# Sixteen narrow tiles in one batch, float16 pairs of queries and keys, and eight weight slots in an encoder trunk

## The chip, the cores and the metric

One Trainium2 chip, one of its cores. The metric is the device time of one execution in microseconds. The engines are named as in the profile: PE (matrix products), DVE (vector), ACT (activations), POOL (GpSimd), SP (issues the DMAs). PEld is PE's loading of the stationary operand, which overlaps with PE.

## The reference

Two layers over 2048 positions of 1024 features. In each layer one input projection feeds a gated spatial mixer (group A) and an attention with eight query heads on two key heads (group B); their outputs together go through one output projection, are normalised and added to x.

```python
for l in range(DEPTH):                                   # DEPTH = 2
    h = rmsnorm(x, pre_g[l])
    proj = jnp.einsum('bsd,de->bse', h, w_in[l])
    u_a, v_a, g_a, q, k, v, g_b = jnp.split(proj, idx, axis=-1)
    y_a = gmlp_group(u_a, v_a, ln_a_g[l], ln_a_b[l], spatial_w[l], spatial_b[l]) * jax.nn.silu(g_a)
    y_b = gqa_axial_attention(q, k, v, q_norm_g[l], k_norm_g[l], tables) * jax.nn.silu(g_b)
    out = jnp.einsum('bse,ed->bsd', jnp.concatenate([y_a, y_b], axis=-1), w_out[l])
    x = x + rmsnorm(out, post_g[l])
# inside the attention, for a block of queries:
    q = apply_axial_rope(rmsnorm(q, qn_g)); k = apply_axial_rope(rmsnorm(k, kn_g))
    sc = jnp.einsum('bqkgd,bskd->bkgqs', qblk, k).astype(jnp.float32) * HEAD_DIM ** -0.5
    p = jax.nn.softmax(sc, axis=-1)
    o = jnp.einsum('bkgqs,bskd->bqkgd', p, v)
```

The inputs' q_norm_g and k_norm_g are drawn around 8, so scores are large and the softmax is sharp.

## The kernel before

Values are kept to nearly float32 by splitting them: a value is the sum of a high and a low part, and a product of two values is made of three products of parts (PASSES). The type float32r, which PE takes at full rate, holds the parts in most places; the attention weights are split into float16 parts.

A layer has two stages. In the **projection stage**, weights come from memory in blocks of 256 columns (load_w, tile w_raw), are scaled and split on ACT and DVE (split_w, tiles w_hi and w_lo), and are multiplied with the transposed input hT. Work that hangs on a block's result is put in a list of delayed jobs (Background) and issued between matmuls: do_kv normalises keys, rotates them and transposes them into k_st and k_lo; do_q does it for queries and stores their two parts to memory (q_d). The pool big holds hT, the keys, the values (v_st) and later the output weights (wo); the pool wp ("w" slots) holds weights, and in the attention p_parts, p_f and y_t; the pool fp ("f" slots) holds tiles of 512 columns.

In the **attention stage** a unit is a block of 512 queries and a head: 32 units a layer, in the order of their blocks. A unit has sixteen steps, one for a tile of 128 keys, so a layer has 512 steps. attend() writes the steps out in one loop over k, and its engines' instructions are kept in that order (Pinned). In step k:

- PE makes the scores sp of tile k from two products: k_st, which holds the keys' high part twice over, with the queries' two parts stacked (s.qs, tile q_st), and k_lo, the keys' low part and a row of ones, with the queries' high part and the row of subtracted maxima (s.q2, tile q2; the order prints it as q_ and a number).
- ACT makes the exponential twice from sp: p_parts (high part, float16) and p_f (float32). POOL, or DVE for 15 of 100 steps, subtracts them to the low part, again p_parts.
- Between, PE makes a maximum product pmax for a later unit (DVE reduces it to mx) and some products of an output projection (pout), which stand in a list called fill.
- PE multiplies the high part of step k - 3 with the values (po, 128 columns of weights), and at the end of every BATCH steps the narrow products of the batch: for each tile two of 32 columns with the low part (po) and two that sum both parts (sums, with one_h). These four stand in different column groups of the array.

The tiles sp, pmax, pout, po, and the small t, pd, pg come from one pool of seven PSUM banks (ps_t). After a unit's last batch, finish() queues what divides by the sums: half and whole join po's two halves (o_pair), den_t and den bring the sums over (den, pd), gate scales the gate gb by them, gate_t and mul apply it, split makes the two parts of y and stores them to y_d.

The maxima only have to be near the true ones, since they divide out; EXP_SHIFT is added to their negative, so that exponentials use float16's range. They go to memory (m_d) as a row of 512.

Of the kernel before, what the change touches and what calls it, by code (L numbers as in the profile page):

```python
# [9 lines left out]
F32 = mybir.dt.float32  # L10
F32R = mybir.dt.float32r
# [27 lines left out]
def encoder(ctx: ExitStack, tc, x, w_in, w_out, pre_g, post_g, ln_a_g, ln_a_b,  # L39
# [18 lines left out]

    def big_t(shape, name):
        return big.tile(shape, F32R, name=name, tag="big")  # L60

# [36 lines left out]
    one_h = const.tile([P, 32], F16, name="one_h")  # L98
    nc.vector.memset(one_h, 1.0)
# [3 lines left out]
    q_d = [dram.tile([NH, 2, HD, GRP], F32, name=f"q_d{g}") for g in range(NG)]  # L103
    m_d = [dram.tile([NH, GRP], F32, name=f"m_d{g}") for g in range(NG)]
    gb_d = [dram.tile([P, TPG, NH * HD], F32, name=f"gb_d{g}") for g in range(NG)]
# [69 lines left out]
    class Project:  # L175
# [23 lines left out]

# [160 lines left out]
        def do_kv(self, g, banks):  # L360
            k_st, k_lo, v32, _ = self.kv
            b4 = [ps.rearrange("p (t h d) -> p t h d", t=2, d=HD) for ps in banks]
            for i, ps in enumerate(b4):
                t = g * TPG + 2 * i
                nc.scalar.copy(v32[:, t:t + 2], ps[:, :, 2:4])
            krs = self.norm_rope([ps[:, :, 0:2] for ps in b4], NKV, self.rope_rows(g, self.gain_k))
            for i, kr in enumerate(krs):
                for j in range(2):
                    t = g * TPG + 2 * i + j
                    kk = f_t("kk", 3 * NKV * HD).rearrange("p (k a d) -> p k a d", k=NKV, a=3)  # L370
                    nc.scalar.copy(kk[:, :, 0, :].bitcast(F32R), kr[:, j])
                    nc.scalar.copy(kk[:, :, 1, :], kk[:, :, 0, :])
                    nc.gpsimd.tensor_tensor(kk[:, :, 2, :], kr[:, j], kk[:, :, 0, :], ALU.subtract)

                    def trans(t=t, kk=kk):
# [4 lines left out]
                        nc.scalar.copy(k_st[:, :, t * P:(t + 1) * P],  # L380
                                       pk[:, 0:2 * P].rearrange("p (k s) -> p k s", k=NKV))
                        nc.vector.tensor_copy(k_lo[0:HD, :, t * P:(t + 1) * P],
                                              pk[0:HD, 2 * P:4 * P].rearrange("p (k s) -> p k s", k=NKV))
                    bg.add(KK_DELAY + 2 * (2 * i + j), trans)

        def do_q(self, g, banks, b):
            qrs = self.norm_rope([ps.rearrange("p (t h d) -> p t h d", t=2, d=HD) for ps in banks], 4,
                                 self.rope_rows(g, self.gain_q))
            for i, qr in enumerate(qrs):
                def trans(i=i, qr=qr):  # L390
                    ps = ps_t("pt").rearrange("p (k t) -> p k t", k=2)
                    for t in range(2):
                        for k in range(2):
                            PE.transpose(ps[:, k, t * P:(t + 1) * P], qr[:, t, 2 * k:2 * k + 2, :], ident)
                    hi = f_t("fh", dt=F32R).rearrange("p (k t) -> p k t", k=2)
                    lo = f_t("fl", dt=F32R).rearrange("p (k t) -> p k t", k=2)
                    nc.scalar.copy(hi, ps)
                    nc.vector.tensor_tensor(lo, ps, hi.bitcast(F32), ALU.subtract)
                    for a, part in enumerate((hi, lo)):
                        for h in range(2):  # L400
                            dst = q_d[g][4 * b + h:4 * b + 4:2, a, :, i * 2 * P:(i + 1) * 2 * P]
                            nc.sync.dma_start(dst.rearrange("k d t -> d k t"),
                                              part.bitcast(F32)[h * HD:(h + 1) * HD])
                bg.add(Q_DELAY + 2 * i, trans)
# [202 lines left out]
    LAG_LO = 3  # L607
    BATCH = 8
    N_HI = 12
    N_F = 4  # L610
    N_LO = 12
    LAST_0 = 5
# [3 lines left out]
    def attend(l, kv, nxt):  # L616
# [31 lines left out]
        def load_qm(u):  # L648
            qb, h = units[u]
            s = state[u]  # L650
            s.qm = f_t("q_m", dt=F32R)
            nc.sync.dma_start(s.qm.bitcast(F32), q_d[qb][h].rearrange("a d t -> (a d) t"))
            s.mx = small.tile([P, TPG, NG], F32, name="mx", bufs=3)

        def load_q(u):
            qb, h = units[u]
            s = state[u]
            s.qs = f_t("q_st", dt=F32R)
            nc.sync.dma_start(s.qs.bitcast(F32), q_d[qb][h].rearrange("a d t -> (a d) t"))
            s.q2 = f_t("q2", dt=F32R)  # L660
            nc.sync.dma_start(s.q2.bitcast(F32)[0:HD], q_d[qb][h, 0])
            nc.sync.dma_start(s.q2.bitcast(F32)[HD:HD + 1], m_d[qb][h:h + 1])

# [13 lines left out]
        def stack_max(u, pe, act):  # L677
# [3 lines left out]
            pe.transpose(ps[0:TPG, 0:P], s.m, ident)  # L681
            rows = small.tile([TPG, P], F32R, name="m_rows")
            act.activation(rows, ps[0:TPG, 0:P], AF.Copy, bias=EXP_SHIFT)
            nc.sync.dma_start(m_d[qb][h].rearrange("(t p) -> t p", p=P), rows.bitcast(F32))

        def finish(u, k):
# [65 lines left out]
            at(k + BATCH + 3, gate_t)  # L752
            at(k + BATCH + 4, mul)
            at(k + BATCH + 5, split)

# [250 lines left out]
        yield before, first_wo  # L1006
        both = [w_t([P, 8, GRP], "p_parts", F16) for _ in range(3)]
        both = [b[:, n] for b in both for n in range(8)]
# [64 lines left out]
        for k in range(end + 4):  # L1073
            if k < total:
                u, i = k // NT, k % NT
                s = state[u]
                kv = units[u][1] // (NH // NKV)
                if i == 0 and units[u][1] % 2 == 0:
                    load_gb(u)
# [30 lines left out]
            if 0 <= kb < total:  # L1110
                u, i = kb // NT, kb % NT
                s = state[u]
                kv = units[u][1] // (NH // NKV)
                if i % BATCH == BATCH - 1:
                    while narrow:
                        narrow.pop(0)()
                    for n in range(i - BATCH + 1, i + 1):
                        kn = kb - i + n
# [7 lines left out]
                if i == NT - 1:  # L1126
                    finish(u, k + 1)
                    if units[u][1] == NH - 1 and u + 1 < len(units):
                        fill_to = min(k + 16 + NH * NT, total - LAST_0)
                        at(k + 16, lambda qb=units[u][0]: fill.extend(out_steps(qb)))  # L1130
        assert not later
# [30 lines left out]
    for l in range(DEPTH):  # L1162
        kv = [big_t([P, NKV, S], "k_st"), big_t([P, NKV, S], "k_lo")]
# [49 lines left out]
```

## Time and profile before

| | us |
|---|---|
| median of three runs | 2810.36 |
| lowest and highest | 2807.75, 2815.12 |
| the profiled execution's own time | 2813.78 |
| its span, first to last instruction | 2812.0 |
| first score product of layer 0 and of layer 1 | 626.7, 2016.5 |
| last score product of layer 0 and of layer 1 | 1388.0, 2773.7 |

The profile is one execution with each instruction's start and end. A row of a list of groups gives the source line (L84 is the helper that records all pinned instructions, so groups are told apart by tiles), the engine, the operation, what it writes and reads, the shapes, how often, the busy time in us, the mean of one in ns, and behind the last bar the idle time of the engine just before them with what ended it. A row of the view in order of time begins with start and duration in us, and merges like instructions that follow each other (x8). The granted clock of PE was 0.99 of full over the execution.

### The profile page before, as it was taken

To read this page: it belongs to the slowest core of one execution; us is meant where nothing else is said; L and a number is where in the kernel's file an instruction comes from. 1 tells how busy PE (TensorE), PEld (TensorE's weight loads), DVE (VectorE), ACT (ScalarE), POOL (GpSimd) and SP (SyncE) were. 2 spreads that over 40 slices of the span, in tenths; PEclk is the share of its full clock that TensorE was granted. 3 is DMA by queue.
4 is the path that set the end of the run, shared out by engine and by line. 5 is a ranking of instruction groups with operands and counts; after the bars stand their busy time and mean duration, and the time that the engine had idled before them with its cause. 6 is when DMAs were issued, how large, how long until landed. Compare 5 with 4: busy or idle time off the path is not lost.

```text
span 2812.0 us, 49354 instructions
## 1 busy us (share of the span) xinstructions
PE 2738.1 (97%) x18294; PEld 2067.2 (74%) x18294; DVE 1894.9 (67%) x3976; ACT 1583.3 (56%) x3295; POOL 1300.1 (46%) x1112
## 2 busy tenths in 40 slices
PE   7999999999999999999999999999999999999997
PEld 7998899885556666566699989998755666666665
DVE  7863788876666666666497639798766555656654
ACT  5322432228887777777642225322478877777774
POOL 1210121018776676666532111200377766767665
PEclk9999999999999999999999999999999999999999
DMA  4533433422222232232345343342322232221323
GB/s 134 165 110 108 137 108 90 124 90 97 85 85 89 94 91 97 87 100 89 139 151 151 122 128 121 102 124 91 112 68 94 78 100 71 83 92 59 115 71 127
DMA packets 276563, 293.71 MB, mean 104 GB/s; under 512 B 20450, under 2 KB 214306, under 8 KB 276324
## 3 DMA queue, kind: packets, MB, share of 16 engines
q1 hardware_dynamic: 276324, 290.57, 33.1%
q8 instruction: 145, 2.38, 0.3%
q14 instruction: 94, 0.77, 0.1%
HBM read 197.02 MB, written 93.45 MB: 103 GB/s over the span
## 4 chain that ended last, share of the span: by engine, by line
PE 79%; DVE 12%; ACT 4%; issue 2%; DMA 1%; POOL 1%; SPq 0%; DVEq 0%; POOLq 0%; ACTq 0%
PE pp L84 25%; PE sp L84 16%; PE pout L84 12%; PE po L84 12%; PE pmax L84 7%; PE sums L84 4%; PE pt L84 2%; DVE fc L346 2%; DVE w_lo L253 2%; ACT p_parts L84 1%; ACT p_f L84 1%; DMA w_raw<-in_w_in_dram 1%; DVE mx L670 1%; DVE o_t L84 1%; DVE fb L435 1%
## 5 line engine op out<-in xcount | busy, mean ns | idle before, releaser
L84 POOL TENSOR_TENSOR p_parts<-p_f,p_parts 128x512 f16<-128x512 f32 x872 | 1038.7, 1207 | 438.9 <-ACT p_f L84 256.7
L84 ACT ACTIVATE p_parts<-sp 128x512 f16<-128x512 f32 x1024 | 627.6, 613 | 334.5 <-PE sp L84 323.1
L84 DVE TENSOR_REDUCE mx<-pmax 128x1 f32<-128x512 f32 x768 | 515.0, 683 | 314.2 <-PE pmax L84 312.3
L84 PE MATMUL po<-p_parts,v_st 128*32 128x512 f16 (+1 forms) x3072 | 638.9, 383 | 0.0
L84 ACT ACTIVATE p_f<-sp 128x512 f32<-128x512 f32 x1024 | 629.3, 615 | 0.0
L84 PE MATMUL sp<-q_st,k_st 128*128 128x512 f32 x1024 | 578.7, 565 | 4.5 <-DVE mx L84 3.5
L84 PE MATMUL pp<-w_hi,hT 128*128 128x256 f32 x3584 | 494.8, 287 | 15.6 <-DVE hT L293 8.1
L84 PE MATMUL pout<-wo,y_t 128*128 128x512 f32 x1488 | 494.2, 397 | 0.0
L84 PEld LDWEIGHTS pp<-w_hi,hT 128*128 128x128 f32 x3584 | 461.1, 194 | 21.9 <-DVE hT L293 8.7
L84 PEld LDWEIGHTS <-v_st 128*32 128x32 f16 (+1 forms) x3072 | 193.0, 96 | 328.6 <-issue 287.4
L84 PE MATMUL pmax<-k_st,q_m 128*128 128x512 f32 x1024 | 409.7, 402 | 5.3 <-DVE mx L84 2.6
L84 PE MATMUL sp<-q,k_lo 65*128 65x512 f32 x1024 | 403.3, 394 | 0.0
L84 PEld LDWEIGHTS pout<-wo,y_t 128*128 128x128 f32 x1488 | 280.3, 189 | 60.8 <-DVE mx L84 1.7
L455 POOL TENSOR_TENSOR fl<-fa,fh 128x512 fp32r<-128x512 f32 x32 | 42.1, 1315 | 516.8 <-ACT fh L454 445.2
L84 PE MATMUL pp<-w_lo,hT 128*128 128x256 f32 x1792 | 262.4, 289 | 2.4 <-DVE w_lo L253 2.2
L84 PE MATMUL pp<-hT,w_hi 128*128 128x512 f32 x1024 | 257.8, 390 | 0.0
L84 PEld LDWEIGHTS sp<-q_st,k_st 128*128 128x128 f32 x1024 | 202.8, 198 | 65.2 <-issue 42.5
L84 PEld LDWEIGHTS pp<-w_lo,hT 128*128 128x128 f32 x1792 | 237.3, 194 | 6.6 <-DVE w_lo L253 4.8
L84 PE MATMUL sums<-p_parts,one_h 128*32 128x512 f16 x2048 | 241.8, 379 | 0.0
L252 ACT ACTIVATE w_hi<-w_raw,g_pre 128x256 fp32r<-128x256 f32 x352 | 151.8, 500 | 153.7 <-DMA w_raw<-in_w_in_dram 108.9
L84 PEld LDWEIGHTS pmax<-k_st,q_m 128*128 128x128 f32 x1024 | 193.4, 189 | 56.7 <-DVE mx L84 4.5
L84 PEld LDWEIGHTS pp<-hT,w_hi 128*128 128x128 f32 x1024 | 191.7, 188 | 39.7
(153 smaller groups left out, 3085.1 us busy)
## 6 DMA issues: line engine op xcount, KB each, us to landing
w_raw<-in_w_in_dram SPq DMA_DIRECT2D x28, 1024.0 KB
y_t<-y_d SPq DMA_DIRECT2D x56, 512.0 KB
w_raw<-in_w_in_dram SPq DMA_DIRECT2D x32, 512.0 KB
q_m<-q_d SPq DMA_DIRECT2D x64, 256.0 KB
q_st<-q_d SPq DMA_DIRECT2D x64, 256.0 KB
x_t<-in_x_dram SPq DMA_DIRECT2D x16, 512.0 KB
q_d<-fh SPq DMA_DIRECT2D x64, 128.0 KB
q_d<-fl SPq DMA_DIRECT2D x64, 128.0 KB
```

Source lines behind the costliest of these rows:

```text
L84: return tc.keep_in_program_order(call(*args, **kw))
L252: nc.scalar.activation(hi[:, d], raw[:, d], AF.Copy, scale=g)
L253: nc.vector.scalar_tensor_tensor(lo[:, d], raw[:, d], g, hi.bitcast(F32)[:, d], ALU.mult, ALU.subtract)
L346: nc.vector.tensor_tensor(t2[:, :, :, lo:lo + 16], qn[:, :, :, hi:hi + 16], tbi[:, :, 1:2, lo:lo + 16].broadcast_to([P, 2, n, 16]), ALU.mult)
L435: nc.vector.scalar_tensor_tensor(s.zt[r, c, :], pz[r, h * P:(h + 1) * P], self.lng[r, c:c + 1], self.zbias[r, c, :], ALU.mult, ALU.add)
L455: nc.gpsimd.tensor_tensor(lo, th, hi.bitcast(F32), ALU.subtract)
L670: dve.tensor_reduce(s.mx[:, j, c:c + 1], ps, AX.X, ALU.max)
```

## The change

Queries and keys are split into float16 parts instead of float32r ones, so q_d, m_d, q_m, q_st, q2 and the keys halve in size. k_st and k_lo become halves of one tile k_t, and the pool big goes from seven to six slots, the pool wp from six to eight. The room in wp goes to p_parts: five tiles instead of three, for 20 high and 20 low parts instead of 12 and 12, and the narrow products come in batches of sixteen tiles (BATCH), except in a layer's last three units (BATCH_END, eight). What finish() queues by the batch's length moves with it, load_gb too, and the output projection's steps enter fill at k + 24 instead of k + 16.

So that the parts fit float16, both gains are divided by a power of two near their largest value (gains). Its product and the factor HEAD_DIM ** -0.5 become a column, unit, by which the exponential scales the scores; EXP_SHIFT becomes a column, shift, which it adds. The keys' low part is now the difference of the transposed key in PSUM and its high part, made by DVE, and no longer transposed by itself; the ones row of k_lo is set by DVE instead of a DMA.

```diff
-    big = ctx.enter_context(tc.tile_pool(name="big", bufs=7))
-    wp = ctx.enter_context(tc.tile_pool(name="wp", bufs=6))
+    big = ctx.enter_context(tc.tile_pool(name="big", bufs=6))
+    wp = ctx.enter_context(tc.tile_pool(name="wp", bufs=8))
...
+    shift = const.tile([P, 1], F32, name="shift")
+    nc.vector.memset(shift, EXP_SHIFT)
...
-            nc.vector.tensor_scalar_mul(self.gain_q, self.gain_q, HD ** -0.5)
+            for i, gain in enumerate((self.gain_q, self.gain_k)):
+                nc.vector.tensor_reduce(top[:, i, 0:1], gain[:, 0], AX.X, ALU.max)
+                nc.vector.tensor_reduce(top[:, i, 1:2], gain[:, 0], AX.X, ALU.min, negate=True)
...
+            for i, gain in enumerate((self.gain_q, self.gain_k)):
+                nc.vector.tensor_scalar(gain, gain, inv[:, i:i + 1], None, ALU.mult)
+            self.unit = lay.tile([P, 1], F32, name="unit", bufs=2)
+            nc.vector.tensor_scalar(self.unit, e[:, 0:1], e[:, 1:2], HD ** -0.5, ALU.mult, ALU.mult)
...
                         for k in range(NKV):
-                            PE.transpose(pk[:, k * P:(k + 1) * P], kk[:, k, 0:2, :], ident)
-                            PE.transpose(pk[0:HD, (2 + k) * P:(3 + k) * P], kk[:, k, 2, :], ident)
+                            PE.transpose(pk[:, k * P:(k + 1) * P], kk[:, NKV * j + k], ident)
...
+                        nc.scalar.copy(k_st[:, :, tt], pk)
+                        nc.vector.tensor_tensor(k_lo[0:HD, :, tt], pk[0:HD], k_st[0:HD, :, tt], ALU.subtract)
...
-    BATCH = 8
-    N_HI = 12
+    BATCH, BATCH_END = 16, 8
+    N_HI = 20
...
-            s.qm = f_t("q_m", dt=F32R)
+            s.qm = f_t("q_m", dt=F16)
...
-            at(k + BATCH, rden)
-            at(k + BATCH + 1, gate)
+            n = batch(u + 1)
+            at(k + n, rden)
+            at(k + n + 1, gate)
             if side == 0:
+                at(k + n - 8, lambda: load_gb(u))
                 return
...
+        def batch(u):
+            return BATCH_END if u >= len(units) - 3 else BATCH
...
-                ACT.activation(p_hi(k), sp, AF.Exp)
-                ACT.activation(p_f(k), sp, AF.Exp)
+                ACT.activation(p_hi(k), sp, AF.Exp, bias=shift, scale=layers[l].unit)
+                ACT.activation(p_f(k), sp, AF.Exp, bias=shift, scale=layers[l].unit)
...
-                if i % BATCH == BATCH - 1:
+                size = batch(u)
+                if i % size == size - 1:
...
-                        at(k + 16, lambda qb=units[u][0]: fill.extend(out_steps(qb)))
+                        at(k + BATCH + 8, lambda qb=units[u][0]: fill.extend(out_steps(qb)))
...
-        nc.sync.dma_start(kv[1].bitcast(F32)[HD:HD + 1].rearrange("p k (n i) -> p (k n) i", i=P),
-                          ones1.unsqueeze(1).broadcast_to([1, NKV * S // P, P]))
+        nc.vector.memset(kv[1][HD:HD + 1], 1.0)
```

ACT's queue where the first layer's attention begins (fa and fh are the last gates of the projection stage, t and m_rows a unit's row of maxima, wo the output weights). Before:

```order
L634 CAST wo<-wo_raw 128x512 x2
L683 ACTIVATE m_rows<-t_7043 4x128
L448 ACTIVATE fa<-pp 128x512
L454 CAST fh<-fa 128x512
L84 ACTIVATE p_parts<-sp 128x512
L84 ACTIVATE p_f<-sp 128x512
```

In the changed kernel:

```order
L646 CAST wo<-wo_raw 128x512 x2
L695 CAST m_rows<-t_6985 4x128
L460 ACTIVATE fa<-pp 128x512
L466 CAST fh<-fa 128x512
L84 ACTIVATE p_parts<-sp,shift,unit 128x512
L84 ACTIVATE p_f<-sp,shift,unit 128x512
```

Nothing moved between them; each exponential reads two more operands, and the row of maxima no longer adds the shift.

PE's queue in the attention, one step and the start of a batch, before:

```order
L84 MATMUL sp<-q_st,k_st 128x512
L84 MATMUL sp<-q_23489,k_lo 128x512
L84 MATMUL pout<-wo,y_t 128x512
L84 LDWEIGHTS v_st
L84 MATMUL po<-p_parts,v_st 128x512
L84 LDWEIGHTS v_st
L84 MATMUL po<-p_parts,v_st 32x512
```

In the changed kernel:

```order
L84 LDWEIGHTS k_t
L84 MATMUL sp<-q_st,k_t 128x512
L84 LDWEIGHTS k_t
L84 MATMUL sp<-q_st,k_t 128x512
L84 MATMUL pout<-wo,y_t 128x512
L84 LDWEIGHTS v_st
L84 MATMUL po<-p_parts,v_st 128x512
L84 MATMUL pd<-den,two_v 32x4 x4
L84 LDWEIGHTS v_st
L84 MATMUL po<-p_parts,v_st 32x512
```

The score products have rows of their own for their weights (float32r products load theirs without one). The last row shown is the first of 32 narrow products (32x512) before, and of 64 now. Over the program 128 batches of 32 become 58 of 64 and 12 of 32.

DVE's queue early in the first layer's projection stage, before:

```order
L283 TENSOR_SCALAR x_t<-x_t,rs_x 128x512 x2
L133 TENSOR_SCALAR rs_m<-ss_x 128x1
L198 TENSOR_SCALAR gain_q<-gain_q 128x128
L134 TENSOR_SCALAR rs_x<-rs_m 128x1
L293 TENSOR_TENSOR hT<-pt,hT 128x4x128
L136 TENSOR_SCALAR rs_t<-rs_x,rs_m 128x1
L253 SCALAR_TENSOR_TENSOR w_lo<-w_raw,g_pre,w_hi 128x256
```

In the changed kernel:

```order
L299 TENSOR_SCALAR x_t<-x_t,rs_x 128x512 x2
L135 TENSOR_SCALAR rs_m<-ss_x 128x1
L1184 MEMSET k_t 1x4096
L136 TENSOR_SCALAR rs_x<-rs_m 128x1
L204 TENSOR_REDUCE g_top<-gain_q 128x1
L138 TENSOR_SCALAR rs_t<-rs_x,rs_m 128x1
L205 TENSOR_REDUCE g_top<-gain_q 128x1
L139 TENSOR_SCALAR rs_x<-rs_t,rs_x 128x1
L206 TENSOR_TENSOR g_exp<-g_top 128x2
L269 SCALAR_TENSOR_TENSOR w_lo<-w_raw,g_pre,w_hi 128x256
```

The ones row (MEMSET k_t) and the work on the gains (g_top and what follows) now stand in DVE's queue ahead of the splits of weights (w_lo) and of the input's low parts (hT) that follow.

More of the change, by code (lines that the diff above doesn't have):

```diff
@@ L57, in encoder, with big_t @@
     dram = ctx.enter_context(tc.tile_pool(name="dram", bufs=1, space=DRAM))
-    def big_t(shape, name):
-        return big.tile(shape, F32R, name=name, tag="big")
+    def big_t(shape, name, dt=F32R):
+        return big.tile(shape, dt, name=name, tag="big")
     def w_t(shape, name, dt=F32R):
@@ L99, in encoder @@
     nc.vector.memset(one_h, 1.0)
+    shift = const.tile([P, 1], F32, name="shift")
+    nc.vector.memset(shift, EXP_SHIFT)
     ws_d = dram.tile([P, 2, NH * P], F32, name="ws_d")
     xn_d = [[dram.tile([P, D], F32, name=f"xn_{l}_{t}") for t in range(NT)] for l in range(DEPTH - 1)]
-    q_d = [dram.tile([NH, 2, HD, GRP], F32, name=f"q_d{g}") for g in range(NG)]
-    m_d = [dram.tile([NH, GRP], F32, name=f"m_d{g}") for g in range(NG)]
+    q_d = [dram.tile([NH, 2, HD, GRP], F16, name=f"q_d{g}") for g in range(NG)]
+    m_d = [dram.tile([NH, GRP], F16, name=f"m_d{g}") for g in range(NG)]
     gb_d = [dram.tile([P, TPG, NH * HD], F32, name=f"gb_d{g}") for g in range(NG)]
@@ L402, in trans @@
                             nc.sync.dma_start(dst.rearrange("k d t -> d k t"),
-                                              part.bitcast(F32)[h * HD:(h + 1) * HD])
+                                              part[h * HD:(h + 1) * HD])
                 bg.add(Q_DELAY + 2 * i, trans)
@@ L657, in load_q @@
             s = state[u]
[L658 to L662, printed above, removed]
+            q = f_t("q_st", 2 * GRP, F16)
+            s.qs, s.q2 = q[:, 0:GRP], q[:, GRP:2 * GRP]
+            nc.sync.dma_start(s.qs, q_d[qb][h].rearrange("a d t -> (a d) t"))
+            nc.sync.dma_start(s.q2[0:HD], q_d[qb][h, 0])
+            nc.sync.dma_start(s.q2[HD:HD + 1], m_d[qb][h:h + 1])
         def max_step(u, n, pe, dve):
@@ L681, in stack_max @@
             pe.transpose(ps[0:TPG, 0:P], s.m, ident)
-            rows = small.tile([TPG, P], F32R, name="m_rows")
-            act.activation(rows, ps[0:TPG, 0:P], AF.Copy, bias=EXP_SHIFT)
-            nc.sync.dma_start(m_d[qb][h].rearrange("(t p) -> t p", p=P), rows.bitcast(F32))
+            rows = small.tile([TPG, P], F16, name="m_rows")
+            act.copy(rows, ps[0:TPG, 0:P])
+            nc.sync.dma_start(m_d[qb][h].rearrange("(t p) -> t p", p=P), rows)
         def finish(u, k):
@@ L1006, in attend @@
         yield before, first_wo
-        both = [w_t([P, 8, GRP], "p_parts", F16) for _ in range(3)]
+        both = [w_t([P, 8, GRP], "p_parts", F16) for _ in range((N_HI + N_LO) // 8)]
         both = [b[:, n] for b in both for n in range(8)]
@@ L1077, in attend @@
                 kv = units[u][1] // (NH // NKV)
-                if i == 0 and units[u][1] % 2 == 0:
-                    load_gb(u)
                 ss = slice(i * P, (i + 1) * P)
@@ L1113, in attend @@
                 kv = units[u][1] // (NH // NKV)
-                if i % BATCH == BATCH - 1:
+                size = batch(u)
+                if i % size == size - 1:
                     while narrow:
                         narrow.pop(0)()
-                    for n in range(i - BATCH + 1, i + 1):
+                    for n in range(i - size + 1, i + 1):
                         kn = kb - i + n
@@ L1162, in encoder @@
     for l in range(DEPTH):
-        kv = [big_t([P, NKV, S], "k_st"), big_t([P, NKV, S], "k_lo")]
+        k_t = big_t([P, 2, NKV, S], "k_t", F16)
+        kv = [k_t[:, 0], k_t[:, 1]]
         v_t = big_t([P, 2, NT * NKV * HD], "v_st")
```

41 lines of the change are left out of this document (22 added, 19 removed).

## The prediction

> **What bounds the kernel now.** I read the page first: its span, the engines' shares and the chain that ended last.
>
> ```profile
> span 2812.0 us, 49354 instructions
> PE 2738.1 (97%) x18294; PEld 2067.2 (74%) x18294; DVE 1894.9 (67%) x3976; ACT 1583.3 (56%) x3295; POOL 1300.1 (46%) x1112
> PE 79%; DVE 12%; ACT 4%; issue 2%; DMA 1%; POOL 1%; SPq 0%; DVEq 0%; POOLq 0%; ACTq 0%
> ```
>
> PE is the bound, and ACT's 56% is a mean over unlike stages. Second view: busy time by stretches, cut at the first and last score product of each layer. The columns are the stretch, its length, and each engine's busy time.
>
> ```profile
> core 0: us, PE busy (x) PEld busy (x) DVE busy (x) ACT busy (x) POOL busy (x), PEclk, DMA share, GB/s
> 626.70:1388.00 761.30, 751.88 (x4958) 465.47 (x4956) 480.62 (x857) 592.36 (x1189) 538.80 (x450) 1.00 0.29 92
> 2016.50:2773.70 757.20, 749.45 (x4958) 464.64 (x4956) 454.70 (x777) 583.96 (x1157) 537.43 (x450) 1.00 0.27 87
> ```
>
> The two attention stages last 761.3 + 757.2 = 1518.5 us, that is 23.73 us for each of the 64 units (a block of queries and a head, sixteen steps). PE is busy 99% of them, but ACT 78%: one fifth is all that ACT can take on. Third, the costliest groups and the waits (us in total, times, longest):
>
> ```profile
> L84 ACT ACTIVATE p_parts<-sp 128x512 f16<-128x512 f32 x1024 | 627.6, 613 | 334.5 <-PE sp L84 323.1
> L84 ACT ACTIVATE p_f<-sp 128x512 f32<-128x512 f32 x1024 | 629.3, 615 | 0.0
> L84 PE MATMUL pmax<-k_st,q_m 128*128 128x512 f32 x1024 | 409.7, 402 | 5.3 <-DVE mx L84 2.6
> L84 POOL TENSOR_TENSOR p_parts<-p_f,p_parts 128x512 f16<-128x512 f32 x872 | 1038.7, 1207 | 438.9 <-ACT p_f L84 256.7
> ACT p_parts L84 <- PE sp L84: 323.1, 352, 2.5
> ```
>
> ACT does two Exps for each of 1024 steps, and its idle time is waiting for scores: today PE leads. Fourth, ACT in order of time, where it runs without waiting:
>
> ```profile
> 1106.34 0.62 ACT L84 ACTIVATE p_f<-sp 128x512 f32<-128x512 f32 x1
> 1106.82 0.63 ACT L84 ACTIVATE p_parts<-sp 128x512 f16<-128x512 f32 x1
> 1107.30 0.65 ACT L84 ACTIVATE p_f<-sp 128x512 f32<-128x512 f32 x1
> 1107.79 0.65 ACT L84 ACTIVATE p_parts<-sp 128x512 f16<-128x512 f32 x1
> 1108.28 0.64 ACT L84 ACTIVATE p_f<-sp 128x512 f32<-128x512 f32 x1
> ```
>
> Starts follow each other by 0.48 to 0.49 us, so a step's pair costs ACT 0.97 us.
>
> **The Exps, the part that decides.** Both Exps now take bias and scale from one-column tiles (shift, unit) instead of from constants. No Exp of before does so, but another ACTIVATE reads its scale from such a tile, v_exp, with the same 512 columns. Here it stands beside a CAST that reads none:
>
> ```profile
> 475.98 1.94 ACT L498 ACTIVATE v_st<-v_st,v_exp 128x512 f16<-128x512 f32 x3
> 477.82 0.61 ACT L422 CAST fh<-fv 128x512 fp32r<-128x512 f32 x1
> 478.33 0.72 ACT L498 ACTIVATE v_st<-v_st,v_exp 128x512 f16<-128x512 f32 x1
> ...
> L498 ACT ACTIVATE v_st<-v_st,v_exp 128x512 f16<-128x512 f32 x8 | 5.3, 711 | 0.0
> L422 ACT CAST fh<-fv 128x512 fp32r<-128x512 f32 x32 | 19.0, 618 | 37.9 <-DVE fv L416 33.3 <-POOL fl L423 4.7
> ...
> L252 ACT ACTIVATE w_hi<-w_raw,g_pre 128x256 fp32r<-128x256 f32 x352 | 151.8, 500 | 153.7 <-DMA w_raw<-in_w_in_dram 108.9 <-DVE w_lo L253 33.8 <-PE sums L84 6.4
> L365 ACT COPY v_st<-pp 128x256 f32<-128x256 f32 x16 | 6.0, 374 | 24.8 <-PE pp L84 24.7
> ```
>
> Back to back, the three with a scale tile take (477.82 - 475.98) / 3 = 0.613 us from start to start, the CAST 0.51: one such operand costs 0.103 us, not hidden by the instruction before. In durations it is 711 - 618 = 93 ns; at 256 columns 500 - 374 = 126 ns. The second operand is in no row. It costs between nothing (both fetched at once) and 0.126. I take 0.103 again, since the only operand seen was paid in full each time, in a row of eight of w_hi as well. So a pair costs 0.97 + 4 x 0.103 = 1.38 us, and ACT's Exps of a unit 22.1 us.
>
> The Trainium skill ("ScalarE: Activation LUTs", under "What ACT_TABLE_LOAD costs") says that an ACTIVATE with immediate scale and bias takes 186 ns + 0.833 ns an element, and that each one-column pointer operand adds about 93 ns. For 512 elements that is 613 ns, as the p_parts row has it, and the 93 ns are those of the two rows above; no run here shows its "each". By the page, with its overlap of 93 ns between neighbours, an Exp would take 706 ns from start to start, and the forecast below would be some 29 us higher.
>
> ACT's other work in a stage is nine groups, in the first stage from
>
> ```profile
> L84 ACT COPY o_pair<-po 64x512 f32<-64x512 f32 x31 | 18.0, 580 | 0.8
> ...
> L84 ACT ACTIVATION_READ_ACCUMULATOR x_r<-o_t 128x1 f32 x16 | 3.3, 203 | 0.0
> ```
>
> with 77.2 us in 166 instructions; less 0.1 each for the overlap that starts show, 1.9 us a unit. The second stage has no x_r and 1.5; mean 1.7. ACT then needs 22.1 + 1.7 = 23.8 us a unit, where the whole unit takes 23.73 today.
>
> **The batches.** PE around one of the batches of eight:
>
> ```profile
> 1108.51 0.39 PE L84 MATMUL sp<-q,k_lo 65*128 65x512 f32 x1
> ...
> 1109.44 0.39 PE L84 MATMUL po<-p_parts,v_st 128*128 128x512 f16 x1
> ...
> 1109.86 0.58 PE L84 MATMUL sums<-p_parts,one_h 128*32 128x512 f16 x4
> 1110.08 0.58 PE L84 MATMUL po<-p_parts,v_st 128*32 128x512 f16 x4
> 1110.29 0.59 PE L84 MATMUL sums<-p_parts,one_h 128*32 128x512 f16 x4
> ...
> 1112.03 0.40 PE L84 MATMUL sp<-q,k_lo 65*128 65x512 f32 x1
> 1112.26 0.40 PE L84 MATMUL pmax<-k_st,q_m 128*128 128x512 f32 x1
> ...
> 1113.43 0.39 PE L84 MATMUL sp<-q,k_lo 65*128 65x512 f32 x1
> ```
>
> Four narrow products run side by side, 0.2155 us a tile (1109.86 to 1110.29 are two tiles). From po at 1109.44 to the score product at 1112.03 pass 2.59 us; less po and the first score product (0.23 each), eight tiles (1.72) and the small pd products (0.1), 0.31 us go into entering and leaving. The order has 128 batches of eight before; now 58 of sixteen and, in each layer's last three units, 12 of eight. 58 fewer are worth 18 us of PE.
>
> But a batch also keeps scores from ACT. From the score product before to the one after pass 1112.03 - 1108.51 = 3.52 us today; with sixteen tiles 5.2. ACT lives meanwhile on scores already there. PE gets two to three steps ahead: po asks for the p_parts of three steps ago, and seven PSUM banks rotate among sp, pmax, po, pout and the rest. Two steps hold 2.98 us of ACT work (1.38 + 0.11 each), three 4.46. So ACT runs dry for 0.7 to 2.2 us a unit; three being the commoner lead, I take 1.3. Before, this cost nothing, since ACT had time to spare.
>
> Unit: 23.8 + 1.3 = 25.1 us, 64 of them 1606 us: 88 us more than 1518.5 (50 to 146 by the two ends of the dry time).
>
> **Float16 products on PE.** Six full products take 1113.43 - 1112.03 = 1.40 us, 0.233 each; a float16 tile of four narrow ones 0.2155. So a score or maximum product in float16 gains between nothing and 0.017 us; I take 0.016, as the narrow rows are the only ones with float16 alone: 2816 in the stages, up to 45 us. With the 18 of the batches PE needs some 1455 us, all of it under ACT's 1606, so both gains buy nothing; they would count if the Exps were cheap. 256 maxima lie in the projections, 4 us there.
>
> **The rest.** Keys lose 64 of 128 transposes, in a stage where PE leads; x4 below is four transposes in 0.60 us with one lasting 0.27, hence 0.11 each: 7 us.
>
> ```profile
> 1116.43 0.60 PE L84 MATMUL pg<-ident,gb 128*128 128x128 f32 x4
> L84 PE MATMUL pt<-ident,kk 128*64 128x128 f32 x64 | 15.7, 272 | 0.0
> L92 DVE MEMSET ones<- 1x128 f32 x1 | 0.2, 165 | 0.8 <-PEq L1200 0.8
> L99 DVE MEMSET one_h<- 128x32 f16 x1 | 0.1, 85 | 0.0
> 28.58 2.93 PE L84 MATMUL pp<-w_hi,hT 128*128 128x256 f32 x12 [4.70 <-DVE hT L293]
> ```
>
> The ones row becomes a DVE MEMSET of 4096 columns: (165 - 85) / 96 = 0.83 ns a column gives 3.4 us a layer (a DMA less on SP against it). It stands ahead of DVE's hT, for which PE already waits 4.70 us at 28.58. With the few short gain operations I count 4 us of it on the path, 0 to 8. POOL loses the subtractions of the keys, q and m transfers halve, two weight slots come free: nothing waits for these at length, and I cost them at nothing. Later load_gb, gate, mul and out_steps go to DVE, PE and SP eight steps later within the same unit rate; nothing else reads them sooner. Sum of the rest: -4 - 7 + 4, about -7.
>
> **Sum.** 2812.0 + 88 - 7 = 2893 us of span. The profiled execution took 2813.8 and the median of the runs is 2810.4, 3.4 less; so 2890 us.
>
> **Rivals.**
> - Both operands are fetched at once, so that the second is free. A pair then costs 0.97 + 2 x 0.103 = 1.18, ACT 20.6 us a unit, and PE stays the bound: 1455 us and some 10 lost behind the longer batches, 2750 in all (2795 if float16 gains nothing). For it: nothing shows a second operand. Against: the first is not hidden. This is the other side; with 1.3 us dry, the second operand decides at 0.06 us: below it faster, above it slower. Chance 0.17.
> - The second costs half, 0.05: pair 1.28, unit 20.5 + 1.7 + 1.3 = 23.5, 2788 us. 0.07.
> - Full price, but ACT never runs dry: 64 x 23.8 = 1523, 2808 us, no change. For it: PE needs less than ACT between batches and can regain its lead. Against: the banks cap that lead under 5.2 us. 0.05.
> - The batch of sixteen waits inside for the last p_lo. Against: po starts when that tile's p_parts is there, p_lo follows a p_f (0.69) and POOL's 1.21 us later, and the last tile's turn comes 15 x 0.2155 = 3.2 us into the batch; costed at nothing.
>
> **How the numbers follow.** My forecast has 0.70, with its own range 2845 to 2955 (dry time 0.7 to 2.2 us, operand 0.09 to 0.126). The range 2760 to 2955 adds the half-priced case and the upper part of the first rival. Slower by over 0.3%, about what a measurement here can tell: 0.72. Faster, the first two rivals: 0.22. Same: 0.06.
>
> **What would show it.** Right: the Exps last about 0.80 us and follow each other by 0.68 to 0.70; ACT is busy over 90% of both attention stages; PE, under 95%, waits for p_parts ahead of po; ACT's waits for sp gather at the batches. Wrong: Exps near 0.71 us and PE still at 99%. The batches' cost shows in the gap between score products around them, near 5.2 us, float16's in six-product steps under 1.40 us where PE does not wait.

## The result, and the profile after

The changed kernel takes 2964.45 us (median of four runs, 2959.79 to 2974.5) where the kernel before takes 2809.06 on the same chip: 1.0554 times as long, with an interval of 1.0522 to 1.0587. It is slower, as forecast, but by 155 us instead of 80, and so lies outside the range of 2760 to 2955.

The head of the page of the changed kernel, with the shares of its chain that ended last:

```profile
span 2963.1 us, 48817 instructions
PE 2744.6 (93%) x18230; PEld 1800.9 (61%) x18230; DVE 1903.6 (64%) x3999; ACT 1897.9 (64%) x3263; POOL 1274.0 (43%) x1080
PE 52%; ACT 26%; DVE 15%; issue 3%; DMA 1%; POOL 0%; SPq 0%; DVEq 0%; ACTq 0%; POOLq 0%
```

PE's share of the chain fell from 79% to 52%, ACT's rose from 4% to 26%. By stretches, cut as before at the first and last score product of each layer:

```profile
core 0: us, PE busy (x) PEld busy (x) DVE busy (x) ACT busy (x) POOL busy (x), PEclk, DMA share, GB/s
627.50:1464.30 836.80, 757.12 (x4958) 351.25 (x4958) 477.89 (x857) 751.42 (x1188) 533.24 (x450) 0.98 0.23 73
2097.40:2925.30 827.90, 757.49 (x4960) 351.95 (x4959) 452.97 (x777) 742.85 (x1157) 532.35 (x450) 0.98 0.22 70
```

The attention stages grew from 1518.5 to 1664.7 us, by 146.2; all the rest of the span grew from 1293.5 to 1298.4, by 4.9. In the stages ACT is busy 90%, PE 91%, and neither is at its limit: a unit of 26.01 us holds 23.35 us of ACT's work, (751.42 + 742.85) / 64, and 2.66 us in which ACT stands idle. The Exps, and what they wait for, from the costliest groups:

```profile
L84 ACT ACTIVATE p_parts<-sp,shift,unit 128x512 f16<-128x512 f32 x1024 | 835.6, 816 | 161.4 <-PE sp L84 159.7
L84 ACT ACTIVATE p_f<-sp,shift,unit 128x512 f32<-128x512 f32 x1024 | 838.3, 819 | 0.0
```

An Exp takes 816 ns instead of 613. ACT's idle time in front of it has halved, from 334.5 to 161.4 us, but now it lengthens the stage, since ACT has no time to spare. Where it arises is seen around a batch of sixteen; ACT first, then PE, in order of time:

```profile
1304.40 0.93 ACT L84 ACTIVATE p_f<-sp,shift,unit 128x512 f32<-128x512 f32 x1
1305.68 0.94 ACT L84 ACTIVATE p_parts<-sp,shift,unit 128x512 f16<-128x512 f32 x1
1306.34 0.94 ACT L84 ACTIVATE p_f<-sp,shift,unit 128x512 f32<-128x512 f32 x1
1307.00 0.95 ACT L84 ACTIVATE p_parts<-sp,shift,unit 128x512 f16<-128x512 f32 x1
1307.66 0.95 ACT L84 ACTIVATE p_f<-sp,shift,unit 128x512 f32<-128x512 f32 x1
1311.14 0.78 ACT L84 ACTIVATE p_parts<-sp,shift,unit 128x512 f16<-128x512 f32 x1 [2.52 <-PE sp L84]
```

```profile
1304.18 0.60 PE L84 MATMUL sp<-q_st,k_t 128*128 128x512 f16 x2
1305.39 0.38 PE L84 MATMUL pmax<-k_t,q_m 128*128 128x512 f16 x1 [0.61 <-ACT p_f L84]
...
1306.93 0.38 PE L84 MATMUL po<-p_parts,v_st 128*32 128x512 f16 x2
...
1310.17 0.39 PE L84 MATMUL po<-p_parts,v_st 128*32 128x512 f16 x2
1310.49 0.61 PE L84 MATMUL sp<-q_st,k_t 128*128 128x512 f16 x2
```

The last score products before the batch start at 1304.18, when ACT begins the p_f at 1304.40. That is all the lead there is: ACT then has two more steps' scores (the four Exps at 1305.68 to 1307.66), and is dry 2.52 us until the scores of 1310.49. Here PE could not take a larger lead: its maximum product at 1305.39 needs a PSUM bank and waits 0.61 us for that p_f of two steps back, which reads a score bank until it ends. Counted from the trace over the 58 batches of sixteen (steps whose p_f has not ended when the last scores before the batch begin), the lead is two steps in 43, three in 9 and one in 6.

### The profile page after: what moved, and what is told of

It reads as the page before. It is cut to its first block, busy times and chain, and to the rows that moved or that the text cites. A ratio compares the mean times of both kernels' runs of the same rounds, so it can differ in the third digit from the quotient of the medians.

```text
span 2963.1 us, 48817 instructions
## 1 busy us (share of the span) xinstructions
PE 2744.6 (93%) x18230; PEld 1800.9 (61%) x18230; DVE 1903.6 (64%) x3999; ACT 1897.9 (64%) x3263; POOL 1274.0 (43%) x1080
## 4 chain that ended last, share of the span: by engine, by line
PE 52%; ACT 26%; DVE 15%; issue 3%; DMA 1%; POOL 0%; SPq 0%; DVEq 0%; ACTq 0%; POOLq 0%
PE pp L84 23%; ACT p_f L84 12%; ACT p_parts L84 11%; PE po L84 7%; PE sp L84 6%; PE pout L84 6%; PE pmax L84 4%; PE sums L84 4%; DVE w_lo L269 2%; DVE fc L362 2%; PE pt L84 2%; DVE o_t L84 1%; DVE mx L84 1%; ACT o_pair L84 1%; DVE fb L447 1%
## 5 line engine op out<-in xcount | busy, mean ns | idle before, releaser
L84 ACT ACTIVATE p_parts<-sp,shift,unit 128x512 f16<-128x512 f32 x1024 | 835.6, 816 | 161.4 <-PE sp L84 159.7
L84 ACT ACTIVATE p_f<-sp,shift,unit 128x512 f32<-128x512 f32 x1024 | 838.3, 819 | 0.0
L84 DVE TENSOR_REDUCE mx<-pmax 128x1 f32<-128x512 f32 x768 | 511.2, 681 | 276.9 <-PE pmax L84 275.2
L84 PE MATMUL pout<-wo,y_t 128*128 128x512 f32 x1488 | 657.4, 508 | 11.3 <-ACT p_f L84 5.0
L84 PE MATMUL sp<-q_st,k_t 128*128 128x512 f16 (+1 forms) x2048 | 623.9, 387 | 38.8 <-ACT p_f L84 27.2
L84 PE MATMUL pmax<-k_t,q_m 128*128 128x512 f16 x1024 | 395.2, 387 | 52.1 <-ACT p_f L84 32.3
L84 PEld LDWEIGHTS <-k_t 128*128 128x128 f16 (+1 forms) x2048 | 197.7, 100 | 234.2 <-issue 127.7
L84 PE MATMUL pp<-hT,w_hi 128*128 128x512 f32 x1024 | 271.7, 413 | 0.0
L84 DVE TENSOR_TENSOR p_parts<-p_f,p_parts 128x512 f16<-128x512 f32 x152 | 111.4, 733 | 179.9 <-ACT p_f L84 179.8
L682 DVE TENSOR_REDUCE mx<-pmax 128x1 f32<-128x512 f32 x256 | 173.4, 686 | 43.9 <-PE pmax L84 41.5
```

Of the source, the lines that this page charges most:

```text
L84: return tc.keep_in_program_order(call(*args, **kw))
L682: dve.tensor_reduce(s.mx[:, j, c:c + 1], ps, AX.X, ALU.max)
```

## The experiments

Times are medians beside the kernel before on the same chip; ratios are to it, with their intervals. "Stage time" is the sum of the two attention stages, "unit" a 64th of it. In these inputs unit is 8.0 in both layers, so a constant 8.0 computes the same. First the two column operands, put into the kernel before, where nothing else is changed:

```diff
-                ACT.activation(p_hi(k), sp, AF.Exp)
-                ACT.activation(p_f(k), sp, AF.Exp)
+                ACT.activation(p_hi(k), sp, AF.Exp, bias=zero_c, scale=unit_c)
+                ACT.activation(p_f(k), sp, AF.Exp, bias=zero_c, scale=unit_c)
```

> The kernel before with nothing but the two columns: bias from a column of zeros, scale from a column of ones, the same numbers out. Operand theory: the Exps last 0.82 us, and with batches of eight and float32r products attention takes 1525 to 1600 us instead of 1518, 2815 to 2895 us in all. Theory that the operands alone make the whole slowdown: 2960 us. Theory that they cost nothing without float16 products: 2810.

Measured 2896.56 us, 1.029 (1.0273 to 1.0307), just above the range of the operand theory and far from the other two. The Exp among the costliest groups, and the two attention stages by stretches:

```profile
L84 ACT ACTIVATE p_parts<-sp,zero_c,unit_c 128x512 f16<-128x512 f32 x1024 | 826.9, 808 | 94.9 <-PE sp L84 93.0
```

```profile
624.80:1427.00 802.20, 773.68 (x4959) 461.85 (x4958) 473.80 (x857) 755.39 (x1189) 536.05 (x450) 1.00 0.27 86
2060.80:2859.10 798.30, 773.12 (x4959) 463.75 (x4958) 450.94 (x777) 745.95 (x1157) 534.05 (x450) 1.00 0.26 81
```

Two columns of zeros and ones, and nothing else, turn ACT's 78% into 94% and make the stages 82 us longer. Even with batches of eight ACT stands idle 1.55 us a unit, (802.20 - 755.39 + 798.30 - 745.95) / 64.

The changed kernel with one operand, and with none:

```diff
-                ACT.activation(p_hi(k), sp, AF.Exp, bias=shift, scale=layers[l].unit)
+                ACT.activation(p_hi(k), sp, AF.Exp, bias=shift, scale=8.0)
```

(the p_f line alike), and in the other run bias=EXP_SHIFT as well.

> The changed kernel with only the bias from a column (scale is the constant 8.0). Operand theory, each operand pays for itself: Exps of about 0.71 us, 0.57 from start to start; PE still leads, 2745 to 2790 us. Theory that one operand costs as much as two: Exps of 0.8 us and 2940 to 2965 us as in the changed kernel.

> The changed kernel with the two columns of the exponentials replaced by constants (bias EXP_SHIFT, scale 8.0, which is the value of unit for these inputs: both gains' largest values lie between 8 and 16, so 8 x 8 x 0.125); batches of sixteen, float16 pairs and the slots stay. Operand theory: the Exps go back to 0.61 us and 0.48 from start to start, ACT needs about 17 us of a unit, PE leads again; attention stages 1447 to 1470 us instead of 1665, 2745 to 2770 us in all, faster than before. Batch theory (long batches starve ACT whatever the Exps cost): 2880 us or more stay.

```profile
L84 ACT ACTIVATE p_parts<-sp,shift 128x512 f16<-128x512 f32 x1024 | 741.4, 724 | 236.3 <-PE sp L84 226.6
```

The row is that with the shift column alone: 2874.53 us, 1.0217 (1.0202 to 1.0232). Durations go 613, 724, 816 ns with none, one and two columns; start to start, where ACT is not held up, 0.48, 0.57 and 0.66 us. Each column is paid, so the theory that both come at once falls; the time came between the two that were expected.

With constants the kernel takes 2827.05 us, 1.0046 (1.0031 to 1.0061): some 140 us go with the columns, but it is still slower than before, and the time lies between the two theories (2770 or less, 2880 or more). What the float16 products and the saved batch switches were to bring did not show. Its stages:

```profile
629.80:1393.40 763.60, 729.39 (x4958) 349.27 (x4958) 485.44 (x857) 587.33 (x1188) 543.83 (x450) 0.99 0.26 81
2028.30:2785.10 756.80, 725.72 (x4960) 347.89 (x4959) 465.56 (x777) 580.14 (x1157) 542.46 (x451) 1.00 0.24 76
```

PE's work in them is 729.39 + 725.72 = 1455.1 us, 46 less than the 751.88 + 749.45 before, but for 65 us PE stands idle, so the batch of sixteen became the suspect. (The prediction's 1455 us is another count: it starts from the stages' whole length and includes the saved switches.) BATCH back to eight, once with the columns and once with constants:

```diff
-    BATCH, BATCH_END = 16, 8
+    BATCH, BATCH_END = 8, 8
```

> The changed kernel with batches of eight throughout; both columns stay. Lead theory (PE gets only about two steps ahead of ACT, so that ACT runs dry by what a batch lasts beyond that): the Exps stay at 0.82 us, ACT's idle time behind a batch goes from 2.0 us to under 0.5, attention 1520 to 1600 us, 2820 to 2900 us. Pure rate theory (ACT's own work sets the time): no change from 2964. Theory that only the number of batches counts (PE's 0.31 us at each): 18 us slower, 2982.

> The changed kernel with constants in the exponentials and batches of eight throughout, so that float16 pairs and the slots are all that is left of the change in the attention. Float16 gain of 0.03 us in a step's median (1.13 against 1.16 us in the run with constants): 64 units x 16 x 0.03 = 31 us less in the stages, some 9 us more elsewhere, 2785 to 2795 us. Rival, that float16 products bring nothing in the stages: 2815 to 2825.

With the columns 2874.30 us, 1.0212 (1.0197 to 1.0227); with constants 2779.33, 0.9887 (0.9871 to 0.9904). The first lies in the range of the lead theory, and the other two theories fall; the second is below the 2785 that was expected. Stages of the first, then of the second:

```profile
631.30:1417.20 785.90, 743.45 (x4959) 342.66 (x4959) 472.84 (x857) 751.15 (x1190) 532.27 (x450) 1.00 0.25 77
2053.20:2833.40 780.20, 741.67 (x4959) 343.22 (x4959) 448.05 (x777) 741.86 (x1157) 530.74 (x450) 1.00 0.24 74
```

```profile
627.70:1369.10 741.40, 727.54 (x4958) 343.27 (x4958) 485.98 (x857) 590.27 (x1190) 536.49 (x450) 1.00 0.26 83
2004.40:2739.90 735.50, 724.07 (x4960) 342.48 (x4959) 461.26 (x777) 581.62 (x1157) 535.01 (x451) 1.00 0.25 79
```

The stage times now form a chain. Its first link holds the float16 pairs and all else that is neither the columns nor the batch; the other two change one thing each, the batch with what is tied to its length: before 1518.5; float16 pairs, batches of eight and constants 1476.9 (-41.6); the two columns 1566.1 (+89.2); batches of sixteen 1664.7 (+98.6). Together +146.2. With the columns ACT's work per unit is the same at both batch lengths, 23.33 and 23.35 us, and its idle time is 1.14 and 2.66: the difference, 1.52 x 64 = 97 us, is nearly the whole last link. Behind each batch ACT is dry 0.44 and 0.52 us with eights (under 0.5 was expected), and 2.04 us a unit with sixteens. With constants the longer batch costs less, 1520.4 - 1476.9 = 43.5 us, but it costs.

Is it the lead that decides how long ACT stays dry? One PSUM bank fewer for the changed kernel:

```diff
-        return psum.tile([P, GRP], F32, name=name, tag="ps", bufs=7)
+        return psum.tile([P, GRP], F32, name=name, tag="ps", bufs=6)
```

> The changed kernel with six rotating PSUM banks instead of seven. Bank theory (the banks cap PE's lead over ACT at about two steps, and ACT runs dry for what a batch lasts beyond that): one bank less is a third of a step less lead, ACT's idle time behind a batch goes from 2.0 to about 2.5 us, 2985 to 3010 us. Rival, PE has no time to regain its lead between batches, or po's wait for p_parts of three steps ago is the cap: 2964, no change.

Measured 3022.48 us, 1.0752 (1.0735 to 1.0769), a little over the upper end; of the 62 us more in the profiled executions 45 are in the attention stages, 17 outside them, which the theory did not speak of.

```profile
636.20:1499.10 862.90, 766.26 (x4958) 350.65 (x4958) 479.36 (x857) 754.94 (x1190) 532.51 (x450) 0.98 0.23 71
2138.80:2986.00 847.20, 761.08 (x4959) 349.77 (x4959) 454.05 (x777) 744.61 (x1157) 531.64 (x450) 0.99 0.22 68
```

ACT's work hardly moves (23.43 us a unit), its idle time goes from 2.66 to 3.29, the part behind the batch from 2.04 to 2.57, as expected. The lead before a batch of sixteen is now one step in 36 of 58 and two in 22, never three. So the number of banks caps the lead. A bank more, the opposite test, was not tried.

What costs 43.5 us where ACT has time to spare? In the run with constants and batches of sixteen, the engines in order of time from the end of a batch on:

```profile
2230.35 0.61 PE L84 MATMUL sp<-q_st,k_t 128*128 128x512 f16 x2
2231.00 0.60 ACT L84 ACTIVATE p_parts<-sp 128x512 f16<-128x512 f32 x1 [2.33 <-PE sp L84]
2232.11 0.58 ACT L84 COPY o_pair<-po 64x512 f32<-64x512 f32 x1
2232.78 0.68 DVE L84 TENSOR_TENSOR o_pair<-po,o_pair 64x512 f32<-64x512 f32 x1 [0.78 <-issue]
2233.38 0.70 DVE L84 STREAM_TRANSPOSE den<-sums 128x512 f32<-128x512 f32 x1
2234.01 0.64 DVE L84 TENSOR_REDUCE mx<-pmax 128x1 f32<-128x512 f32 x1
2234.59 0.72 DVE L84 TENSOR_TENSOR gb<-gb,rden 128x256 f32<-128x256 f32 x1
2235.57 0.63 PE L84 MATMUL pg<-ident,gb 128*128 128x128 f32 x4 [2.00 <-DVE gb L84]
```

The gate of a unit moved by eight steps, to just behind the next unit's batch. There DVE's queue holds first that unit's join of po's halves, which waits for ACT's copy, which stands behind Exps that the batch made late; then den, mx, and only then gb, and PE waits 2.00 us with pg. In all 26 such waits of over 0.3 us in this run, pg starts 0.06 to 0.26 us behind the end of gb. The gate was moved five steps on, out_steps behind it; once with the columns, and once with constants and the ones row by a DMA, as before (the last three lines belong to this second run alone):

```diff
-            at(k + n + 3, gate_t)
-            at(k + n + 4, mul)
-            at(k + n + 5, split)
+            d = 5 if n == BATCH else 0
+            at(k + n + 3 + d, gate_t)
+            at(k + n + 4 + d, mul)
+            at(k + n + 5 + d, split)
...
-                        at(k + BATCH + 8, lambda qb=units[u][0]: fill.extend(out_steps(qb)))
+                        at(k + BATCH + 13, lambda qb=units[u][0]: fill.extend(out_steps(qb)))
...
-        nc.vector.memset(kv[1][HD:HD + 1], 1.0)
+        nc.sync.dma_start(kv[1][HD:HD + 1].rearrange("p k (n i) -> p (k n) i", i=P),
+                          ones_h.unsqueeze(1).broadcast_to([1, NKV * S // P, P]))
```

> The changed kernel, columns and all, with only the gate's transposes, product and split and the output projection's steps five steps later. Collision theory: step 6 of a unit (2.28 us in the changed kernel) loses 0.7 to 0.9 us, but ACT sets the pace, so that only what ACT idled for it comes back (0.4 us a unit in steps 7 and 8): 2930 to 2945 us. Rival, the collision is in ACT's shadow: 2964.

> The run with constants (batches of sixteen), in which the transposes of the gate, its product and its split are queued five steps later, the output projection's steps too, and the ones row is set by a DMA again. Collision theory: the gate's work on DVE now stands behind the next unit's join of po's halves, which waits for a copy on ACT behind the long batch, so that PE waits at the gate's transposes (step 6 of a unit: 1.93 us against 1.13 of its neighbours); five steps later PE waits no more, step 6 goes to 1.2, the transposes' step to 1.6, 40 to 60 us off the stages. MEMSET theory: the other stages lose 6 to 8 of their 1302 us. Together 2760 to 2785 us, faster than before. Rival, that batches of sixteen cost what they save for another reason: 2815 to 2827.

With the columns 2958.65 us, 1.0529 (1.0513 to 1.0544), near the rival's 2964: ACT's idle time at steps 7 and 8 fell from 0.35 to 0.08 us a unit, but that behind the batch grew from 2.04 to 2.18. With constants 2807.51, 0.999 (0.998 to 0.9999), less gained than expected. From the trace, the mean time from one step's first score product to the next one's, in us:

| step of the unit | 2 (batch) | 6 | 10 | 11 | all sixteen |
|---|---|---|---|---|---|
| sixteen, constants | 4.74 | 1.93 | 1.36 | 1.29 | 23.79 |
| the same, gate later | 4.72 | 1.24 | 1.39 | 1.48 | 23.52 |
| eight, constants | 2.99 | 1.16 | 3.24 | 1.21 | 23.11 |

(Step 10 holds the second batch in the last row. Each mean also holds a layer's first unit, which has no batch at step 2, and its last three, whose batches are of eight in every kernel.) The saved switch is there: in the 28 units between, the two steps with batches of eight last 3.06 + 3.26 us, the one with a batch of sixteen and step 10 without one 4.99 + 1.14, 0.19 less (0.30 by medians). The gate's transposes stand at step 6, at step 11 in the second row and at step 14 in the third, where that step lasts 1.45; so most of what step 11 shows is their own work, which only moved. What step 6 lost is PE's idle time, 0.44 us a unit there and 0.02 with the gate later. That is 27 us, but stage time falls only by 17.4, to 1503.0, since other waits grew; 26 remain over the batch of eight. PE's waits for DVE's maxima (mx, m_neg) are 26.8 us in the stages of the second row, 13.9 in those of the third.

Last, whether those 26 us hang on DVE's queue: in that kernel all low parts to POOL.

```diff
-    SHARE_0 = 15
-    SHARE = 15
+    SHARE_0 = 0
+    SHARE = 0
```

> The kernel with batches of sixteen, constants, the gate five steps later and the ones row by DMA (2807.5 us), with all low parts subtracted on POOL, none on DVE (the 15 of 100 that DVE did). Theory, what is left of the loss at batches of sixteen is PE waiting for DVE, whose queue is held up behind the batch: DVE loses 0.15 x 16 = 2.4 subtractions a unit, the waits for m_neg and mx shrink, the attention stages go from 1502.9 towards 1485, the time to 2785 to 2798 us. Rival, it is POOL's p_lo or ACT's p_f: POOL then has 16 x 1.21 = 19.4 us of subtractions in a unit of 23.5 us, p_lo comes later, p_f's and PE's waits grow: 2810 us or more.

Measured 2794.99 us, 0.9948 (0.9929 to 0.9967), within the theory's range, but the stages of the profiled execution fell only by 4.8 us, to 748.9 + 749.3. The sums over both stages, first of the kernel with the gate later, then of this one:

```profile
sum 1503.00, PE 1453.48 PEld 697.12 DVE 951.40 ACT 1166.30 POOL 1083.52; mean PE 726.74 PEld 348.56 DVE 475.70 ACT 583.15 POOL 541.76
sum 1498.20, PE 1452.25 PEld 698.90 DVE 840.99 ACT 1164.10 POOL 1224.84; mean PE 726.13 PEld 349.45 DVE 420.50 ACT 582.05 POOL 612.42
```

PE has three new waits of over 5 us there. POOL, DVE and PE at one of them, in order of time:

```profile
2193.90 7.83 POOL L84 TENSOR_TENSOR p_parts<-p_f,p_parts 128x512 f16<-128x512 f32 x7
```

```profile
2195.63 6.38 DVE L84 TENSOR_TENSOR gb<-gb,rden 128x256 f32<-128x256 f32 x1
```

```profile
2202.66 0.59 PE L84 MATMUL pmax<-k_t,q_m 128*128 128x512 f16 x1 [5.40 <-DVE mx L84]
```

gb, 0.41 us by itself, ends 0.28 us after POOL's row of seven subtractions is over (2193.90 + 7.83 = 2201.73). PE's idle time in the stages is 1503.00 - 1453.48 = 49.5 us with the gate later and 46.0 here, and 16.1 of these are the three new waits. Without them it would be some 30 us, an estimate, against 25.3 with batches of eight. By this estimate most of the remaining loss hangs on DVE's queue, and a fuller POOL brings a new one; no run has the relief without the new waits.

The best parts together: float16 pairs, batches of eight, constants, the ones row by a DMA, and gains that are not divided, so that the factor is the constant HEAD_DIM ** -0.5 whatever the inputs. This leaves out what lets the parts fit float16 with larger gains; the times are for these inputs.

```diff
-    BATCH, BATCH_END = 16, 8
+    BATCH, BATCH_END = 8, 8
...
-            for i, gain in enumerate((self.gain_q, self.gain_k)):
-                nc.vector.tensor_scalar(gain, gain, inv[:, i:i + 1], None, ALU.mult)
...
-                ACT.activation(p_hi(k), sp, AF.Exp, bias=shift, scale=layers[l].unit)
+                ACT.activation(p_hi(k), sp, AF.Exp, bias=EXP_SHIFT, scale=HD ** -0.5)
```

> Batches of eight and constants in both Exps as in the run that took 2779 us, but the gains are not divided by powers of two (the Exps' constant scale is then HEAD_DIM ** -0.5, with no column to be made), and the ones row of k_lo comes by a DMA from a float16 row again. If the 4096-column MEMSET (3.47 us a layer) and the operations on the gains stood on PE's path into the projection stages, 5 to 10 us go: 2769 to 2775 us, ratio 0.984 to 0.988. Rival, they stood beside other waits: 2777 to 2782 us. The attention stages stay at 741 and 735 us either way.

Measured 2775.46 us, 0.9877 (0.9862 to 0.9892), the lowest median of all and just above the upper end of what was expected. Its stages are unchanged, 740.2 + 735.6; what is outside them fell by 5 us in the profiled executions (1300.6 to 1295.7). The medians differ by 3.9 us, and the intervals of the two ratios overlap.

## Why the prediction was right and wrong

- **What bounds the kernel.** Right: PE bound it, and ACT could take on a fifth. Two columns alone made the kernel before 3% slower.
- **The Exps.** Right, and a little high: each of the two operands costs 0.09 us, 0.66 from start to start instead of 0.69. ACT's work is 23.35 us a unit against 23.8: 29 us less than summed. The Trainium skill's price in "ScalarE: Activation LUTs" ("What ACT_TABLE_LOAD costs") is about 93 ns for each pointer operand; the trace agrees to a tenth, with (816 - 613) / 2 = 102. The estimate of 706 ns from start to start, worked out from the figures of that page of the Trainium skill, does not hold: starts are 0.66 us apart here.
- **The dry time.** This is the step that failed. 1.3 us were taken, from three steps of lead as "the commoner"; the trace has two in 43 of 58 batches, capped by the banks, and 2.66 us of idle time a unit. By steps of the unit, 2.04 of it stand directly behind the batch, inside the 0.7 to 2.2 given, and some 0.6 elsewhere, 0.35 of this at steps 7 and 8, just behind the moved gate, which no term had. 1.36 x 64 = 87 us too little. The Exps, taken 29 us too high, hid a third of that, which was luck. po's wait for p_parts was named as a cap and as the thing to see; by the waits (us in total, times, longest) it is small, and PE waits for p_f, which holds the banks:

```profile
PE pmax L84 <- ACT p_f L84: 32.3, 55, 1.4
PE sp L84 <- ACT p_f L84: 27.2, 59, 1.0
PE po L84 <- ACT p_parts L84: 4.7, 17, 0.3
```

Before, PE hardly waited for it:

```profile
PE pmax L84 <- ACT p_f L84: 0.9, 3, 0.4
PE sp L84 <- ACT p_f L84: 0.4, 2, 0.2
```

- **The gap.** Right: 5.2 us were expected from the second score product before a batch to the second behind it, and over the 58 batches of sixteen it is 5.30 on mean, 5.10 by the median. The batch was not longer than thought; the lead was shorter.
- **Costed at nothing, and not nothing.** "The same unit rate" held for the gate, but it came to stand behind a join that waits. With constants it is worth some 17 us of the stages; with the columns the stages fell by 1.6 us and the medians by 6, within their intervals.
- **Float16.** Right: -41.6 us where up to 45 was given (with all else of the first link), and invisible under ACT, as said. The saved switches are there too, 0.19 to 0.30 us each where 0.31 was taken, so 11 to 17 us instead of 18, and were more than lost to the waits behind the longer batch.
- **The rest.** -7 us expected, +4.9 measured. The ones row among the groups lasts as worked out, and among the waits is PE's for hT in the second layer, first in the changed kernel, then before:

```profile
L1184 DVE MEMSET k_t<- 1x4096 f16 x2 | 6.9, 3472 | 1.8 <-issue 1.8
```

```profile
PE pt L84 <- DVE hT L84: 4.9, 1, 4.9
PE pt L84 <- DVE hT L84: 0.5, 1, 0.5
```

The wait for hT in the first layer grew too, from 4.70 to 6.94 us. The last run took 5 us back by removing the ones row and the work on the gains from DVE. Of the 11 us that fewer transposes and float16 maxima were to bring outside the stages, 6.7 show in PE's work, (2738.1 - 1501.3) - (2744.6 - 1514.6), but PE's idle time there grew by 11.6; the two waits for hT are 6.6 of it, what makes up the other 5 was not followed.

Against the profiled span: -29 (Exps) + 87 (dry) + 12 (rest) = 70 us, from 2893 to 2963. The rivals with a cheap second operand fell by the run with one column, and the one in which ACT never runs dry by the 2.04 us behind the batch. The one with a wait for the last p_lo inside the batch falls too: among PE's waits none is for POOL's p_parts. What first made the cheap operand look so good, 2750 us with PE as the bound, was wrong by itself: with constants the changed kernel needs 2827, so at no price of an operand would the change as a whole have been faster.

## What to carry to other kernels

Before an engine with a fifth to spare gets more work, price the work by its rows, and then treat every interruption of its feed anew: a pause of a few microseconds that was free under slack is paid in full. How much of it can be bridged is set by the buffers between the two engines, here PSUM banks that are released two steps back, and one looks for the instruction that waits for the buffer rather than for the one that waits for the data. Steps that are tied to a batch's length move with it, and should be looked at where they land: here it was behind a long batch, where DVE's queue ran late.

## What the hardware showed that was not expected

DVE's product of two SBUF tiles, gb, takes 0.41 us on average (at most 0.43) where it starts while POOL is idle, and 1.02 where it starts beside a subtraction of POOL (50 of 64 in the changed kernel; up to 1.39). It does not always wait only for the one in progress: with all low parts on POOL and its subtractions back to back, it waited for that and the five that followed, 6.38 us, twice. The Trainium skill ("SBUF — State Buffer", "Summary: rules for kernel authors") says that a DVE operation with two SBUF inputs and a GpSimd operation that reads SBUF block each other, the second until the first has finished; the runs agree, and add that others which come after may go ahead.
